# Conditioning products in pairs, and fp32 products of 512 columns cut in two

## The chip, the cores and the metric

The kernel runs on one core of a Trainium2 chip, in one launch. The metric is the device time of that launch in microseconds. TensorE (PE) multiplies; DVE, ACT and POOL work element by element; SP issues most transfers between HBM and the core's memory.

## The reference

A two-layer diffusion backbone on 256 latent and 256 context tokens of width 1024. Layer 0 mixes state-space heads and eight attention heads, layer 1 is a gated MLP over chunks; each is followed by an expert network that picks 16 of 16384 experts for each of eight heads of each token. A conditioning vector gives shift, scale and gate of every sub-layer:

```python
sh1, sc1, g1, sh2, sc2, g2 = jnp.split((cond_lat @ ada_w[layer] + ada_b[layer])[:, None, :], N_MOD, axis=-1)
h_l = _modulate(_rmsnorm(x, norm1_g[layer]), sh1, sc1)
...
x = x + g1 * y_l
x = x + g2 * _peer(_modulate(_rmsnorm(x, norm2_g[layer]), sh2, sc2), ...)
```

`ada_w` is 2 x 1024 x 6144 in fp32, 50 MB, and only two rows (latent and context condition) are multiplied with it.

## The kernel before, in words

The parts follow each other: layer 0's mixer (products into convolution, states and low-rank projections; then attention and state-space outputs; then the output projection), its experts, layer 1's gated MLP, its experts. All heavy products run on TensorE. Large weights come in fp32 tiles `wr` through SP's queue, are split into a high and a low part (`whl`) on ACT and on POOL or DVE, and multiplied in three passes (`mm3`); other products are plain fp32 (`mm`, line 250). A plain fp32 product shows in the profile as two records, each with its own weight load.

The conditioning products are spread through layer 0's mixer. Four tiles `aw` (line 50, `NAW = 4`; 128 x 512, 256 KB each) take turns. `ada_group` (line 494) makes one group of 2048 of the 6144 columns of a layer: 8 slices of the inner dimension (k) by 4 column tiles (t), 32 products, each a tile `aw` against the condition's slice `condT[:, k, :]` of 32 columns. The result of column tile t goes into rows 32t to 32t + 31 of one bank, `ps`, so the four tiles of a k use four different strips of rows. A step issues the transfer of tile i and then multiplies tile i - 3. `adas` (line 728) runs five groups one after the other: group (0,1), (0,2), (1,0), (1,1), (1,2), as (layer, group), all into the same bank; between two groups `ada_tail` adds the bias on DVE, from the bank into `mod` or `mt`. The first group, (0,0), has code of its own: `ada_first`, and `second`, whose last four products read `aw` too. So 164 products read `aw`.

The order on every engine is written when the program is built, by a planner (`schedule`, line 206): each part of the work is a generator that yields conditions; a clock for each engine (`Clock`) adds up costs, and of the generators that are ready the one goes on whose engine's clock is lowest; among equals the first of the list. `at(...)` (line 246) is ready when TensorE's clock has come to the time at which the tiles are there. `ada` is the third of the first list (the mixer's input part) and the first of the second list (attention). Since all clocks are shared, a shift in one place can move work on every engine behind it. Instructions of an engine run in the written order: one that waits holds all that stand behind it on its engine.

In the attention part, four passes work on two heads each. `scores` makes the keys (`kn`, products of `ckh` and `ckl`), the values (`vt`), the queries (`qn`, and `qr` with a rotation on DVE), then for two heads and two token halves the scores, a product of 512 columns with `kn` and one with `krT` into one bank. DVE takes the row maximum (`mx`), ACT the exponential (`pe`), DVE scales it. `values` transposes `pe` (to `pT`) and multiplies it with `vt`. In between, `segments` and `weights` build the state-space part's decay matrices on DVE, eight operations of 128 x 128 at a time (`seg` with `mask_f` or `mask_b`, then `MT`, then `seg` with `dt`), and `outputs` uses them. Eight banks (`pa` and `pb`, four each) go round; a bank that is taken again must have been read.

Plain fp32 products of 512 columns into 128 rows are: the scores, the states (`xw`), the state-space outputs (`hc` and `hs` with `bcT`), broadcasts of one row of `mod`, and in the expert part the products of the rows that tokens share (`rows` with `sc`).

Of the kernel before, what the change touches and what calls it, by code (L numbers as in the profile page):

```python
# [10 lines left out]
F32 = mybir.dt.float32  # L11
# [9 lines left out]
P = 128  # L21
D = 1024
KD = 8
# [174 lines left out]
def tile_backbone(ctx: ExitStack, tc: tile.TileContext, a: dict, out: bass.AP):  # L198
# [3 lines left out]
    clock = Clock()  # L202
    clk = clock.at
    T, V, S, G, Q = (Engine(e, n, clock) for e, n in ((nc.tensor, "T"), (nc.vector, "V"), (nc.scalar, "S"), (nc.gpsimd, "G"), (nc.sync, "D")))
# [28 lines left out]
    class Banks:  # L233
# [5 lines left out]
        def get(self):  # L239
            self.free.sort(key=clock.idle)  # L240
            return self.free.pop(0)
# [4 lines left out]
    def at(*aps):  # L246

        return lambda: clk["T"] + SLACK >= max(clock.ready(x) for x in aps)

    def mm(o, lhsT, rhs, start=True, stop=True):  # L250
        T.matmul(o, lhsT, rhs, start=start, stop=stop)

    def mm3(o, lh, ll, rh, rl, start=True, stop=True):
# [37 lines left out]
    condT = cp.tile([P, KD, 32], F32, name="condT")  # L291
# [120 lines left out]
    def warm(ps, x):  # L412

        while clk["T"] + WARM < clock.ready(x):
            mm(ps[:, :256], identb, ones.bitcast(F16))
# [61 lines left out]
    def features(hh, hl, A, SH, raws):  # L477

        pss, idle = [pa() for _ in range(KD // 2)], pb()
        for t in range(2):  # L480
            warm(idle, diag[t])
            for j in range(KD):
                mm(pss[j // 2][:, j % 2 * 256 + t * P:j % 2 * 256 + (t + 1) * P], xt[t][:, j * P:(j + 1) * P], diag[t])
        for j in range(KD):
            ps, raw, h = pss[j // 2][:, j % 2 * 256:(j % 2 + 1) * 256], raws(j), hh[:, j, :]
            S.activation(h, ps, AF.Identity, scale=A[:, j, 0:1], bias=SH[:, j, 0:1])
            V.tensor_scalar(raw, ps, A[:, j, 0:1], SH[:, j, 0:1], op0=ALU.mult, op1=ALU.add)
            (G if j % 3 == 2 else V).tensor_tensor(hl[:, j, :], raw, h.bitcast(F32), op=ALU.subtract)


    def ada_tail(m, ps):
        V.tensor_tensor(m, ps, m, op=ALU.add)

    def ada_group(l, g, get, bufs, ps):

        units = [(k, t) for k in range(KD) for t in range(4)]
        n = len(bufs)
        for i in range(len(units) + n - 1):
            if i < len(units):
                k, t = units[i]  # L500
                aw = bufs[i % n]
                yield lambda: clk["T"] >= clock.idle(aw)
                Q.dma_start(out=aw, in_=a["ada_w"][l, k * P:(k + 1) * P, g * 2048 + t * 512:g * 2048 + (t + 1) * 512])
            if i >= n - 1:
                k, t = units[i - n + 1]
                aw = bufs[(i - n + 1) % n]
                yield at(aw)
                mm(ps[32 * t:32 * t + 32, :], condT[:, k, :], aw, k == 0, k == KD - 1)
        ada_tail(get(), ps)
        yield  # L510

# [86 lines left out]
    def hybrid(mod):  # L598
# [129 lines left out]
        def adas():  # L728

            yield lambda: "mod1" in done  # L730
            ps = B.get()
            for l, g in ((0, 1), (0, 2), (1, 0), (1, 1), (1, 2)):
                if l == 0:
                    mod.append(mod_load(0, g))
                    yield from ada_group(l, g, lambda: mod[g], awb, ps)
                    done.add(("mod", g))
                    if g == 2:
                        mod2(0, mod, awb[0])
                elif g == 0:
                    yield from ada_group(l, g, lambda: nmod.append(mod_load(1, 0)) or nmod[0], awb, ps)  # L740
                else:
                    mt = ha.tile([P, 512], F32, name="mt", tag="mt")
                    yield from ada_group(l, g, lambda: mod_load(1, g, mt), awb, ps)
                    if g == 2:
                        mod2(1, [None, None, mt], awb[0])
                    S.dma_start(out=ms[g - 1], in_=mt)
            B.put(ps)
# [1383 lines left out]
```

## Time and profile before

| | |
|---|---|
| median of 3 runs | 2077.2 us (2073.23 to 2078.44) |
| the profiled execution | 2073.34 us |
| its span, first to last instruction | 2071.6 us |
| TensorE busy | 1945.0 us, 94% of the span |
| DVE busy | 1368.5 us, 66% |
| landing tiles `aw`: products, records | 164, 328 |
| TensorE idle until a transfer into `aw` had landed | 8.0 us, 11 times |

A profile shows one execution. TensorE's products show as records of which the next may start before the last has ended, so the distance of starts tells what one costs, and the length does not. In the names, `out<-in` stands for what is written and read; for a product the moving operand comes first, then the one held in the array, and 128*32 is the shape of the held operand.

### The profile page before, as it was taken

How to read it: one execution, taken by the hardware profiler on the slowest of the kernel's cores; microseconds unless marked ns; L12 is line 12 of the kernel's file. 1: busy time of each engine (PE TensorE's matmuls, PEld its weight loads, DVE VectorE, ACT ScalarE, POOL GpSimd, SP SyncE). 2: the span in 40 equal slices, each digit the busy share in tenths (PEclk: the TensorE clock that was granted, in tenths of full speed). 3: DMA queues.
4: the chain of work that ended last, by engine and by line, in shares of the span. 5: the costliest groups of instructions: out<-in, count | busy, mean ns of one | idle time of the engine just before them, and what ended most of it. 6: DMA issues, size and time to landing. Idle time of an engine off the chain costs nothing.

```text
span 2071.6 us, 28401 instructions
## 1 busy us (share of the span) xinstructions
PE 1945.0 (94%) x10048; PEld 1574.3 (76%) x10048; DVE 1368.5 (66%) x3634; ACT 540.4 (26%) x1386; POOL 592.2 (29%) x378
## 2 busy tenths in 40 slices
PE   7899999999989999998999998999899999989997
PEld 4565444579878888887877788789688888878786
DVE  3575566247988678878664226579888887776651
ACT  4434343344212122210111154442122221101100
POOL 1324222166011112223221188550111112233210
PEclk9999999999989999999999999999999999989999
DMA  8556664555468668998997364454678788989972
GB/s 302 171 184 215 212 217 145 165 173 184 133 225 293 237 220 310 379 378 293 417 410 260 132 234 153 156 191 128 229 283 307 269 297 298 365 295 412 413 274 82
DMA packets 132489, 519.98 MB, mean 251 GB/s; under 512 B 17222, under 2 KB 17414, under 8 KB 107179
## 3 DMA queue, kind: packets, MB, share of 16 engines
q1 hardware_dynamic: 100320, 312.24, 43.2%
q0 software_dynamic: 30720, 204.69, 25.9%
q8 instruction: 79, 1.29, 0.2%
q10 hardware_dynamic: 1296, 1.15, 0.2%
q14 instruction: 74, 0.61, 0.1%
HBM read 525.60 MB, written 6.91 MB: 257 GB/s over the span
## 4 chain that ended last, share of the span: by engine, by line
PE 55%; DVE 19%; issue 12%; DMA 7%; POOL 5%; ACT 2%; POOLq 0%; SPq 0%; ACTq 0%; DVEq 0%
PE pb L169 28%; PE pa L169 27%; DVE ge L169 6%; DMA wr<-in_dn 4%; POOL rows L169 2%; DVE mk L169 2%; POOL whl L169 2%; DVE acc L169 1%; DVE junk L169 1%; DMA acs<-acc 1%; DVE rows L169 1%; DMA rows<-in_uv,gidx 1%; DVE x L169 1%; DVE oc L169 1%; DVE cacc L169 0%
## 5 line engine op out<-in xcount | busy, mean ns | idle before, releaser
L169 PE MATMUL pa<-phf,wr 128*128 128x256 f32 x2560 | 576.1, 386 | 0.0
L169 PE MATMUL pb<-wr,ge 128*128 128x256 f32 x2560 | 569.4, 383 | 6.5 <-DMA wr<-in_dn 5.4
L169 PEld LDWEIGHTS pb<-wr,ge 128*128 128x128 f32 x2560 | 485.2, 191 | 90.3 <-DMA wr<-in_dn 22.9
L169 PEld LDWEIGHTS pa<-phf,wr 128*128 128x128 f32 x2560 | 492.3, 194 | 67.2
L169 POOL DMA_INDIRECT rows<-in_uv,gidx x200 | 231.7, 1158 | 916.8 <-DVE acc L169 608.0
L169 POOL TENSOR_TENSOR whl<-wr,whl 128x1024 fp32r<-128x1024 f32 (+2 forms) x130 | 314.7, 2434 | 401.9 <-ACT whl L169 392.2
L169 DVE SCALAR_TENSOR_TENSOR junk<-rows,h 128x1024 bf16<-128x1024 f32 x200 | 244.0, 1220 | 85.6 <-DMA rows<-in_uv,gidx 82.5
L169 DVE SCALAR_TENSOR_TENSOR acc<-rows,wt,acc 128x1024 f32<-128x1024 f32 x196 | 250.7, 1279 | 0.0
L169 ACT ACTIVATE act<-act 128x1 f32<-128x1 f32 x206 | 41.7, 203 | 435.6 <-DVE junk L169 420.6
L169 ACT CAST whl<-wr 128x1024 fp32r<-128x1024 f32 (+2 forms) x136 | 136.9, 1018 | 70.7 <-PE pa L169 27.7
L169 ACT ACTIVATE sg<-pa 128x256 f32<-128x256 f32 (+25 forms) x126 | 38.8, 308 | 383.9 <-PE pa L169 375.4
L169 PE MATMUL pb<-oc,o 128*128 128x80 f16 x1024 | 88.2, 255 | 31.8 <-DVE oc L169 31.8
L169 PEld LDWEIGHTS <-o 128*128 128x128 f16 x1024 | 80.8, 118 | 40.9 <-DVE o L169 16.3
L169 PE MATMUL pa<-phh,whl 128*128 128x256 f32 x512 | 96.3, 285 | 2.1 <-DVE phf L169 2.1
L169 PE MATMUL pb<-aw,condT 128*32 128x512 f32 x328 | 93.4, 624 | 5.1 <-DVE mod L169 3.0
L169 DVE SCALAR_TENSOR_TENSOR ge<-pb,ge 128x80 f32<-128x80 f32 (+29 forms) x128 | 36.9, 316 | 78.3 <-ACT ge L169 77.2
L169 PEld LDWEIGHTS pa<-phh,whl 128*128 128x128 f32 x512 | 80.8, 191 | 4.0 <-DVE phf L169 2.5
L169 PE MATMUL pa<-phl,whl 128*128 128x256 f32 x256 | 73.2, 286 | 2.4 <-POOL phl L169 1.3
L169 DVE SCALAR_TENSOR_TENSOR mk<-jp,j,gte 128x128 f32<-128x128 f32 x256 | 72.4, 347 | 1.1
L169 PE MATMUL pb<-whl,cath 128*128 128x512 f32 x192 | 61.8, 400 | 2.0 <-POOL whl L169 1.1
L169 ACT ACTIVATE wt<-act,gsel 128x1 f32<-128x1 f32 x200 | 58.9, 295 | 6.5
L169 DVE TENSOR_TENSOR oc<-eq,pkT 128x640 f16<-128x640 f16 x128 | 57.1, 487 | 2.2
(517 smaller groups left out, 2402.0 us busy)
## 6 DMA issues: line engine op xcount, KB each, us to landing
wr<-in_dn SPq DMA_DIRECT2D x320, 512.0 KB
aw<-in_ada_w SPq DMA_DIRECT2D x164, 256.0 KB
wr<-in_wq SPq DMA_DIRECT2D x32, 512.0 KB
wr<-in_w_out SPq DMA_DIRECT2D x16, 512.0 KB
wr<-in_gm_w_v SPq DMA_DIRECT2D x16, 512.0 KB
wr<-in_gm_w_u SPq DMA_DIRECT2D x16, 512.0 KB
wr<-in_gm_w_out SPq DMA_DIRECT2D x16, 512.0 KB
wr<-in_w_xbc SPq DMA_DIRECT2D x12, 512.0 KB
```

The costliest lines, as they stand in the source:

```text
L169: return f(*args, **kw)
```

## The change

`mm` cuts a plain fp32 product of 512 columns into 128 rows into two of 256 columns of the same bank. `ada_group` goes in steps of two: it waits until two tiles have landed, multiplies both, and then issues the next two transfers into the same two tiles. Two pairs take turns.

```diff
     def mm(o, lhsT, rhs, start=True, stop=True):
+        if rhs.dtype == F32 and lhsT.dtype == F32 and len(rhs.shape) == 2 and rhs.shape[1] == 512 and o.shape[0] == P:
+
+            T.matmul(o[:, :256], lhsT, rhs[:, :256], start=start, stop=False)
+            T.matmul(o[:, 256:], lhsT, rhs[:, 256:], start=False, stop=stop)
+            return
         T.matmul(o, lhsT, rhs, start=start, stop=stop)
...
-        for i in range(len(units) + n - 1):
+        for i in range(0, len(units) + n, 2):
+            if i >= n:
+
+                yield at(*bufs[i % n:i % n + 2])
+                for j in range(2):
+                    k, t = units[i - n + j]
+                    mm(ps[32 * t:32 * t + 32, :], condT[:, k, :], bufs[i % n + j], k == 0, k == KD - 1)
             if i < len(units):
-                k, t = units[i]
-                aw = bufs[i % n]
-                yield lambda: clk["T"] >= clock.idle(aw)
-                Q.dma_start(out=aw, in_=a["ada_w"][l, k * P:(k + 1) * P, g * 2048 + t * 512:g * 2048 + (t + 1) * 512])
-            if i >= n - 1:
-                k, t = units[i - n + 1]
-                aw = bufs[(i - n + 1) % n]
-                yield at(aw)
-                mm(ps[32 * t:32 * t + 32, :], condT[:, k, :], aw, k == 0, k == KD - 1)
+                yield lambda: clk["T"] >= max(clock.idle(x) for x in bufs[i % n:i % n + 2])
+                for j in range(2):
+                    k, t = units[i + j]
+                    Q.dma_start(out=bufs[i % n + j], in_=a["ada_w"][l, k * P:(k + 1) * P, g * 2048 + t * 512:g * 2048 + (t + 1) * 512])
```

The conditioning products themselves, into 32 rows, stay whole. A conditioning group is 16 pairs. What the planner makes of it is seen at three places. The numbers behind the names are those of the built program and differ between the two.

TensorE, second pair of heads, before: conditioning products (`condT`) between the scores (`kn`, `krT`), the transposes (`ident`) and others.

```order
L169 MATMUL pb_127<-aw3_326,condT_82 32x512
L169 MATMUL pb_127<-aw0_323,condT_82 32x512
L169 MATMUL pb_127<-aw1_324,condT_82 32x512
L169 MATMUL pa_124<-kn_1914,qn_2116 128x512
L169 MATMUL pa_124<-krT_336,qr_2173 128x512
L169 MATMUL pb_127<-aw2_325,condT_82 32x512
L169 MATMUL pb_128<-kn_1914,qn_2116 128x512
L169 MATMUL pb_128<-krT_336,qr_2173 128x512
L169 MATMUL pb_129<-ident_69,yt_2043 128x128 x4
L169 MATMUL pb_130<-kn_1914,qn_2116 128x512
L169 MATMUL pb_130<-krT_336,qr_2173 128x512
L169 MATMUL pa_123<-ident_69,pe_2205 128x128 x4
```

The same engine and pair after the change:

```order
L169 MATMUL pb_127<-aw2_325,condT_82 32x512
L169 MATMUL pb_127<-aw3_326,condT_82 32x512
L169 MATMUL pa_123<-kn_1991,qn_2141 128x256 x2
L169 MATMUL pa_123<-krT_336,qr_2223 128x256 x2
L169 MATMUL pa_124<-ident_69,yt_2072 128x128 x4
L169 MATMUL pb_127<-aw0_323,condT_82 32x512
L169 MATMUL pb_127<-aw1_324,condT_82 32x512
L169 MATMUL pb_129<-hs0_329,bcT_339 128x256 x2
L169 MATMUL pa_125<-hc1_328,bcT_339 128x256 x2
L169 MATMUL pb_130<-xlat_337,MT_2094 128x64 x8
L169 MATMUL pb_127<-aw2_325,condT_82 32x512
L169 MATMUL pb_127<-aw3_326,condT_82 32x512
```

Before, runs of three, one and, a few rows later, one; after, each run holds two products, and scores are two instructions each (x2).

DVE, first pair of heads, before: from the rotation of the queries (`qrt`, `qr`) to the first scores' scaling (`pe`).

```order
L169 TENSOR_TENSOR qrt_1809<-pa_123,c2_332 128x256 x2
L169 TENSOR_TENSOR qr_1810<-qrt_1809 128x256
L169 SCALAR_TENSOR_TENSOR seg_1668<-seg_1668,dt_340,cbT_1658 128x128 x8
L169 TENSOR_TENSOR yt_1825<-xlat_337,c2_332 128x512
L169 TENSOR_TENSOR yo_1828<-pa_125,ecum_344 128x512
L169 TENSOR_TENSOR yt_1825<-yt_1825,yo_1828 128x512
L169 TENSOR_TENSOR yo_1834<-pa_126,ecum_344 128x512
L169 TENSOR_TENSOR yt_1825<-yt_1825,yo_1834 128x512
L169 TENSOR_REDUCE mx_1839<-pa_124 128x1
L169 TENSOR_SCALAR mx_1839<-mx_1839 128x1
L169 RECIPROCAL sm_1843<-sm_1843 128x1
L169 TENSOR_SCALAR pe_1842<-pe_1842,sm_1843 128x512
```

DVE after the change, from the first of the additions behind the rotation to the first maximum:

```order
L169 TENSOR_TENSOR yt_1831<-xlat_337,c2_332 128x512
L169 TENSOR_TENSOR yo_1835<-pa_126,ecum_344 128x512
L169 TENSOR_TENSOR yt_1831<-yt_1831,yo_1835 128x512
L169 TENSOR_TENSOR yo_1840<-pb_130,ecum_344 128x512
L169 TENSOR_TENSOR yt_1831<-yt_1831,yo_1840 128x512
L169 SCALAR_TENSOR_TENSOR seg_1727<-seg_1727,cum_341,mask_f_146 128x128 x8
L169 SCALAR_TENSOR_TENSOR seg_1857<-seg_1857,cum_341,mask_b_150 128x128 x8
L169 SCALAR_TENSOR_TENSOR MT_1871<-seg_1727,dt_340,cbT_1666 128x128 x8
L169 SCALAR_TENSOR_TENSOR seg_1857<-seg_1857,dt_340,cbT_1666 128x128 x8
L169 SCALAR_TENSOR_TENSOR seg_1869<-seg_1869,cum_341,mask_f_146 128x128 x8
L169 SCALAR_TENSOR_TENSOR seg_1899<-seg_1899,cum_341,mask_b_150 128x128 x8
L169 TENSOR_REDUCE mx_1917<-pa_123 128x1
```

Between the additions to `yt` and the first maximum six blocks of eight operations (x8) have come in, which stood behind the pair's maxima before.

TensorE, first pair of heads, before: the first scores' bank was `pa_124`, as the maximum's row on DVE shows; here it is taken again, by a key product of the next pair.

```order
L169 MATMUL pa_123<-ident_69,pe_1842 128x128 x4
L169 MATMUL pa_125<-kn_1678,qn_1753 128x512
L169 MATMUL pa_125<-krT_336,qr_1810 128x512
L169 MATMUL pb_127<-aw0_323,condT_82 32x512
L169 MATMUL pb_127<-aw1_324,condT_82 32x512
L169 MATMUL pa_126<-ident_69,pe_1856 128x128 x4
L169 MATMUL pb_127<-aw2_325,condT_82 32x512
L169 MATMUL pa_124<-ckh_335,whl_1750 128x512
L169 MATMUL pa_124<-ckl_334,whl_1750 128x512
L169 MATMUL pa_124<-ckh_335,whl_1750 128x512 x2
L169 MATMUL pa_124<-ckl_334,whl_1750 128x512
L169 MATMUL pa_124<-ckh_335,whl_1750 128x512
```

After the change the first scores' bank is `pa_123` (the maximum's row), and a value product of the next pair takes it:

```order
L169 MATMUL pa_126<-ckh_335,whl_1748 128x512
L169 MATMUL pa_126<-ckl_334,whl_1748 128x512
L169 MATMUL pa_126<-ckh_335,whl_1748 128x512 x2
L169 MATMUL pa_126<-ckl_334,whl_1748 128x512
L169 MATMUL pa_126<-ckh_335,whl_1748 128x512
L169 MATMUL pb_130<-ckh_335,whl_1748 128x512
L169 MATMUL pb_130<-ckl_334,whl_1748 128x512
L169 MATMUL pb_130<-ckh_335,whl_1748 128x512 x2
L169 MATMUL pb_130<-ckl_334,whl_1748 128x512
L169 MATMUL pb_130<-ckh_335,whl_1748 128x512
L169 MATMUL pa_123<-whl_1748,ckh_335 128x256 x2
```

Before, two transposes of `pe` and a run stood ahead of the bank's next use; after, the value product takes the bank ahead of the first transpose.

## Rows read from the trace of the kernel before

**Rows 1.** The page: busy time by engine; the chain that ended last, by engine.
```profile
PE 1945.0 (94%) x10048; PEld 1574.3 (76%) x10048; DVE 1368.5 (66%) x3634; ACT 540.4 (26%) x1386; POOL 592.2 (29%) x378
PE 55%; DVE 19%; issue 12%; DMA 7%; POOL 5%; ACT 2%; POOLq 0%; SPq 0%; ACTq 0%; DVEq 0%
```

**Rows 2.** Stretches: length; busy us of PE, PEld, DVE, ACT, POOL; clock; DMA.
```profile
230.00:300.00 70.00, 68.17 (x310) 34.31 (x308) 51.72 (x138) 30.83 (x54) 15.85 (x7) 1.00 0.66 220
300.00:396.00 96.00, 91.38 (x395) 44.74 (x396) 48.74 (x115) 34.39 (x70) 19.65 (x8) 0.98 0.53 173
```

**Rows 3.** TensorE's timeline: start, length, what, shape, count; key products and one run.
```profile
260.74 0.63 PE L169 MATMUL pa<-ckh,whl 128*128 128x512 f32 x2
...
261.44 0.40 PE L169 MATMUL pa<-ckh,whl 128*128 128x512 f32 x1
261.77 1.05 PE L169 MATMUL pb<-aw,condT 128*32 128x512 f32 x2
262.75 0.50 PE L169 MATMUL pb<-ckh,whl 128*128 128x512 f32 x1
263.08 0.40 PE L169 MATMUL pb<-ckl,whl 128*128 128x512 f32 x1
```

**Rows 4.** TensorE's timeline: a run of four products, eight records.
```profile
109.28 1.06 PE L169 MATMUL pb<-aw,condT 128*32 128x512 f32 x8
110.28 0.50 PE L169 MATMUL pa<-hh,whl 128*128 128x512 f32 x1
```

**Rows 5.** TensorE's timeline: 512 columns, 256 columns, and 256 between other shapes.
```profile
1129.99 10.46 PE L169 MATMUL pb<-rows,sc 128*128 128x512 f32 x24
...
555.71 19.59 PE L169 MATMUL pa<-phf,wr 128*128 128x256 f32 x90
...
312.63 1.99 PE L169 MATMUL pb<-pT,vt 128*128 128x256 f32 x8
314.56 1.05 PE L169 MATMUL pb<-aw,condT 128*32 128x512 f32 x4
```

**Rows 6.** DVE's timeline in the first attention pair, and ACT's exponential.
```profile
231.13 2.19 DVE L169 SCALAR_TENSOR_TENSOR seg<-seg,cum,mask_f 128x128 f32<-128x128 f32 x8 [2.19 <-DMA seg<-cums]
...
249.33 0.68 DVE L169 TENSOR_REDUCE mx<-pa 128x1 f32<-128x512 f32 x1
...
251.65 0.68 DVE L169 TENSOR_REDUCE mx<-pb 128x1 f32<-128x512 f32 x1
...
250.24 0.69 ACT L169 ACTIVATE pe<-pa,mx 128x512 f32<-128x512 f32 x1 [11.19 <-DVE mx L169]
```

**Rows 7.** TensorE's timeline in the first attention pair.
```profile
244.04 1.02 PE L169 MATMUL pa<-kn,qn 128*128 128x512 f32 x2
...
246.04 1.05 PE L169 MATMUL pb<-aw,condT 128*32 128x512 f32 x4
247.03 1.12 PE L169 MATMUL pb<-kn,qn 128*128 128x512 f32 x2
...
249.13 1.13 PE L169 MATMUL pb<-kn,qn 128*128 128x512 f32 x2
...
252.22 2.00 PE L169 MATMUL pb<-xlat,MT 128*128 128x64 f32 x16
254.15 1.05 PE L169 MATMUL pb<-aw,condT 128*32 128x512 f32 x4
```

**Rows 8.** TensorE's timeline: waits, with what ended them in brackets.
```profile
128.72 2.02 PE L169 MATMUL pb<-aw,condT 128*32 128x512 f32 x8 [3.05 <-DVE mod L169]
...
163.75 1.05 PE L169 MATMUL pb<-aw,condT 128*32 128x512 f32 x2 [0.31 <-DMA aw<-in_ada_w]
...
347.60 1.12 PE L169 MATMUL pa<-ident,pe 128*128 128x128 f32 x4 [4.62 <-DVE pe L169]
...
1841.10 0.56 PE L169 MATMUL pa<-cnt,tri 128*128 128x1 f32 x2 [8.83 <-DVE cnt L169]
```

**Rows 9.** SP's timeline: issues to the landing tiles ahead of 163.75.
```profile
160.78 1.75 SPq L169 DMA_DIRECT2D aw<-in_ada_w  x4
```

## The prediction

> **What bounds the kernel now.** I read the page's busy shares and its chain first [rows 1]: TensorE is busy for 94% of the span and makes 55% of the chain; no other engine is above 66%. Then the table of stretches [rows 2]: in the two stretches of the attention part TensorE is busy for 68.2 of 70 us and 91.4 of 96 us, DVE for 51.7 and 48.7, at full granted clock (1.00, the 2.4 GHz level) or 0.98. There the conditioning products of the change stand, between 42 us and 394 us. A microsecond of TensorE work taken out of this part shortens the kernel by a microsecond, as long as no other engine holds TensorE up in its place.
>
> What such a product costs I read from TensorE's timeline. A product of 512 fp32 columns into 32 rows shows as two records. In a stream of products that start 0.23 us apart, (261.44 - 260.74) / 3 with one record left out between, one alone (two records) pushes the stream apart [rows 3]: from the product at 261.44 to that at 263.08 pass 1.64 us, of which two steps of 0.235 us belong to the stream, so the run costs 1.17 us (0.98 from its start to the next product's, 0.19 in slower steps ahead of it and behind it). Two products in a row (four records) take 0.99 us, from 246.04 to 247.03 [rows 7], and four (eight records) 1.00 us [rows 4]: they write four different strips of 32 rows and stream at the same time. So **runs** are paid for, and not products.
>
> **The change, part by part.**
>
> *Fewer runs.* On TensorE's order before, the 164 products that read the four landing tiles stand in 82 runs, 27 of them a single product; after the change in 69, with one single (the last of the second() part, which is not touched). By group of 32 products: 12, 12, 19, 20 and 17 runs before, 11, 11, 13, 16 and 16 after, and two ahead of them in both. 13 runs less x 1.17 us = **-15.3 us**. Removed runs beside other work that waits would give less, but TensorE hardly idles in this part: of its 82 runs the tables of waits show a handful next to one [rows 8].
>
> *The 512-column products cut in two.* The condition takes fp32 products into 128 rows with 512 columns: 24 of the shared rows, 32 of the scores, 20 of the states and their outputs (12 + 8), 16 broadcasts of one row, 92 in all, 184 records. Back to back, 24 records of the shared rows come at (10.46 - 0.59) / 23 = 0.4291 us; records of 256 columns at (19.59 - 0.38) / 89 = 0.2158 us [rows 5]; the subtracted part is the last record's own length. Two of these make 0.4316, 2.5 ns more than one of 512: 184 x 2.5 ns = **+0.5 us**. Weight loads double (184 more), but one of a 256-column stream lies within the record ahead of it, else the step would not be 0.216. Where another tile shape follows, the scores take 2.10 us for two products, or 1.05 each, and four products of 256 columns in the same surroundings 1.93 us, or 0.97 for two [rows 5, 7]; so the bounds are -92 x 0.08 = -7.4 us and, if each extra weight load stood free for the 0.1 us by which a stream is set back at a switch [rows 3], +18.4 us. I take +0.5, from the rows that show the form itself.
>
> The Trainium skill, TensorEngine Tiling (Array Packing), section Instruction Overhead, says that each matmul carries about 60 cycles; at 2.4 GHz that is 25 ns, an estimate of 4.6 us for 184 more records, and the sum below would come to -9.3. The two cadences of this trace contradict it.
>
> *A moved wait on DVE.* The planner's clocks shift, and DVE's order in the first attention pair changes: six blocks of eight seg or MT operations now stand ahead of the first row maximum, where none stood. A block takes 2.18 us [rows 6], six 13.1 us. In the times of before: the maximum began at 249.33 and the exponential of it ended at 251.0, 1.7 us later; now it begins at 262.4 and ends at 264.1. TensorE's order does not wait for it at a transpose but at a bank: after the change the value product takes the bank of the first scores, pa_123. The first scores began at 244.04; one run less stands ahead, so 243.0. From there to the value product: a score pair 2.1, a run 1.1, a pair 2.1, eight MT products 1.9, a run 1.1, two pairs 4.2, twelve key products at 0.235, 2.8 [rows 3, 7]: 258.3. It waits 5.8 us. The third scores' bank is asked for at 264.1 + 1.4 + 1.1 + 0.5 + 1.1 + 0.5 = 268.7 (values, run, transposes, run, transposes); each later maximum comes 2.32 us after the last [rows 6] and two additions lie between, 0.7 each like the maximum, which reads as many columns, so its exponential ends at 264.1 + 4.6 + 1.4 = 270.1: 1.4 us. The next conditioning group must wait for the addition that empties its bank, which stands on DVE behind the fourth maximum (262.4 + 3 x 2.32 + 1.4 = 270.8, its scores ready at 273.1), a weight subtraction of 768 columns (1.0, by columns) and three copies of 512 (0.7 each): it ends at 276.9, and TensorE is there at 270.1 + 1.4 + 1.1 + 0.5 + 1.9 = 275.0 (values, run, transposes, two state products): 1.9 us. Queued behind each wait is all of TensorE. Together **+9.1 us**. From below it is 0 (DVE gets ahead earlier: it idles for 18 of 70 us in this stretch), from above 13.1, the whole of the six blocks.
>
> *Waits that go.* The run at 128.72 waited 3.05 us for the addition of its group [rows 8]; now 24 products at 0.235 and eight transposes at 0.11 stand between the two groups, 6.5 us. At 347.60 TensorE waited 4.62 us for a maximum that came behind the last seg block and additions; that block now comes before the pair's scores, so the last maxima stand behind two additions only. **-7.7 us**, between 0 and that. The waits for landing tiles (0.31 us at 163.75 [rows 8]) I leave as they are: one transfer a product stays, into the same four tiles.
>
> *The weights' transfers* move on SP's queue behind other aw transfers; by TensorE's work between the run that frees the last aw tile ahead of one and its first use, no weight of this part has less than about 20 us, before or after. Cost 0; the cover is those 20 us, and without it a weight's way through the queue, ACT and POOL would show. Later stages: the one-hot products of the expert part move by a product or so; DVE is the one waited for there, and the wait at the listing (8.83 us in the second layer [rows 8]) takes up what is lost ahead of it. Cost 0, bounds -5 and +5.
>
> Sum: -15.3 + 0.5 + 9.1 - 7.7 = -13.4. The profiled execution took 2073.3 us (span 2071.6 and 1.7 around it), so 2059.9; the median of the runs shown is 3.9 us above the profiled execution, which puts the forecast at **2064 us**.
>
> **Rivals.** *None of the old waits goes.* TensorE is faster now and meets the same DVE results later in its own work; a wait at the bank or at the transposes takes the place of each. For it: the DVE wait at 347.60 arose just as the new one does. Against: DVE's own order ahead of the last maxima is shorter. -15.3 + 0.5 + 9.1 = -5.7, and 2071.5: no change that can be told.
>
> *The pair waits for its second half.* A run may start when both halves have landed, and both are issued only when the run that used the tiles is over. Before, the run at 163.75 still waited although its transfer was issued at about 161 [rows 8, 9]. If each of the 45 runs of the last three groups waits 0.5 us, that is 22.5 us: -13.4 + 22.5 = +9, and 2086, slower. From 0.3 us a run it eats the gain. Against: the 45 runs lie over some 166 us, 3.7 us apart, and a tile is used again two runs later, 7.4 us.
>
> *The moved DVE work costs nothing.* If DVE begins its six blocks early enough, the +9.1 falls out: -22.5, and 2055. Against: the blocks stand behind the rotation of the queries, which needs TensorE's last query product.
>
> **How the numbers follow.** 0.60 for the forecast (2058 to 2070 its own range), 0.17 for the old waits that stay, 0.09 for the waits on second halves, 0.14 for the free DVE work. 0.3% is 6.2 us, about what a measurement of this kernel can tell from no change. Faster: 0.14 and nearly all of 0.60, 0.72; within it: the rest of that and 0.17, 0.19; slower: 0.09. The range goes from the last rival to just past no change: 2053 to 2079.
>
> **What would show it.** TensorE's timeline with 69 runs on the landing tiles, a single one among them, each 0.98 us; records of 256 columns of rows,sc at 0.216 us. A wait of some 6 us on ACT pe or DVE at the first value products of the second pair, and none at the last scores. Wrong it is if the summed idle time of TensorE up to 400 us grows by more than 10 us, if waits for aw are above 10 us in all (8.0 before), or if a score pair takes clearly more or less than 2.1 us.

## The result, and the profile after

The changed kernel takes 2065.65 us (median of 6 runs, 2063.17 to 2067.31) against 2076.97 us (6 runs, 2072.95 to 2078.44): ratio 0.9949, 95% interval 0.9936 to 0.9962, or 11.3 us less. The forecast was 2064. The profiled execution took 2064.5 us, with a span of 2062.8. (The granted clock in the tables is a share of full speed: 1.00 is the 2.4 GHz level, 0.50 the 1.2 GHz level.)

The page after, busy time and the chain by engine (before: [rows 1]):

```profile
PE 1935.5 (94%) x10229; PEld 1606.4 (78%) x10229; DVE 1370.5 (66%) x3635; ACT 542.2 (26%) x1380; POOL 596.5 (29%) x377
PE 62%; DVE 17%; DMA 8%; issue 7%; POOL 4%; ACT 2%; SPq 0%; POOLq 0%; ACTq 0%; DVEq 0%
```

TensorE has 181 more records and 9.5 us less busy time. Stretches after the change: busy us of PE, PEld, DVE, ACT and POOL, then granted clock and DMA (before: [rows 2]).

```profile
230.00:300.00 70.00, 60.26 (x303) 37.37 (x301) 55.42 (x153) 28.89 (x51) 22.58 (x7) 0.93 0.58 195
300.00:396.00 96.00, 92.28 (x469) 56.36 (x469) 41.38 (x92) 36.90 (x76) 15.49 (x7) 0.99 0.57 188
```

In the first stretch, where TensorE was busy for 68.2 of 70 us, it is now busy for 60.3, at a clock of 0.93: something new stands in its way there. TensorE's timeline, runs and a split score pair at another place, and the split products of the shared rows (before: [rows 3, 5, 7]):

```profile
300.38 1.05 PE L169 MATMUL pb<-aw,condT 128*32 128x512 f32 x4
301.36 1.13 PE L169 MATMUL pb<-kn,qn 128*128 128x256 f32 x4
302.42 1.13 PE L169 MATMUL pb<-krT,qr 64*128 64x256 f32 x4
303.48 1.05 PE L169 MATMUL pb<-aw,condT 128*32 128x512 f32 x4
304.46 0.66 PE L169 MATMUL pa<-ident,pe 128*128 128x128 f32 x4
...
1116.28 10.52 PE L169 MATMUL pb<-rows,sc 128*128 128x256 f32 x48
```

A pair of conditioning products (x4 records) costs 0.98 us, from 300.38 to 301.36, as a single one did; there are 69 runs. A score pair takes 303.48 - 301.36 = 2.12 us, 2.10 before. 48 records of 256 columns come at (10.52 - 0.38) / 47 = 0.2157 us, as forecast.

TensorE in the first attention pair (before: [rows 7]), with what ended a wait in brackets:

```profile
251.71 0.39 PE L169 MATMUL pb<-ckh,whl 128*128 128x512 f32 x1
258.05 0.80 PE L169 MATMUL pa<-whl,ckh 128*128 128x256 f32 x2 [5.95 <-ACT pe L169]
...
264.38 2.59 PE L169 MATMUL pb<-aw,condT 128*32 128x512 f32 x4 [3.40 <-DMA aw<-in_ada_w]
266.89 1.11 PE L169 MATMUL pa<-ident,pe 128*128 128x128 f32 x4
```

DVE's blocks ahead of the first maximum, from the first to the last of the six and the maximum (before: [rows 6]):

```profile
243.65 2.18 DVE L169 SCALAR_TENSOR_TENSOR seg<-seg,cum,mask_f 128x128 f32<-128x128 f32 x8
...
254.15 2.18 DVE L169 SCALAR_TENSOR_TENSOR seg<-seg,cum,mask_b 128x128 f32<-128x128 f32 x8
256.25 0.68 DVE L169 TENSOR_REDUCE mx<-pa 128x1 f32<-128x512 f32 x1
```

The value product of the second pair waits 5.95 us for the exponential that frees its bank: the wait that was forecast, with 5.8, at the place in the order that was forecast. Behind it, in this execution, comes one that was not: 3.40 us for a landing tile (the runs below show that it does not come each time). SP's own queue over the same time, and what it waited for:

```profile
236.32 0.80 SPq L169 DMA_DIRECT2D aw<-in_ada_w  x2
237.18 21.71 SPq L169 DMA_DIRECT2D seg<-cums  x4
258.98 1.80 SPq L169 DMA_DIRECT2D aw<-in_ada_w  x4
```
```profile
SPq L169 <- POOL MT L169: 12.3, 2, 8.1
SPq L169 <- DVE MT L169: 7.8, 1, 7.8
```

The six blocks bring four seg transfers with them, which stand in a row on SP. Three of these wait, 20.1 us in sum, until an older seg tile has been read, and the conditioning transfers stand behind them until 258.98.

The two waits that were to go are gone: where runs waited 3.05 and 4.62 us [rows 8], the timeline after the change shows no wait in the runs at 130.70 and 137.48 and in the transposes at 347.93.

### The profile page after: what moved, and what is told of

It is laid out like the page before. It is cut to its first block, busy times and chain, and to the rows that moved or that the text cites. A ratio compares the mean times of both kernels' runs of the same rounds, so it can differ in the third digit from the quotient of the medians.

```text
span 2062.8 us, 28777 instructions
## 1 busy us (share of the span) xinstructions
PE 1935.5 (94%) x10229; PEld 1606.4 (78%) x10229; DVE 1370.5 (66%) x3635; ACT 542.2 (26%) x1380; POOL 596.5 (29%) x377
## 4 chain that ended last, share of the span: by engine, by line
PE 62%; DVE 17%; DMA 8%; issue 7%; POOL 4%; ACT 2%; SPq 0%; POOLq 0%; ACTq 0%; DVEq 0%
PE pa L169 32%; PE pb L169 30%; DVE ge L169 6%; DMA wr<-in_dn 6%; POOL whl L169 2%; DVE mk L169 1%; POOL rows L169 1%; DVE rows L169 1%; DVE acc L169 1%; DVE junk L169 1%; DMA aw<-in_ada_w 1%; DVE x L169 1%; DMA acs<-acc 1%; DVE oc L169 1%; DVE seg L169 0%
## 5 line engine op out<-in xcount | busy, mean ns | idle before, releaser
L169 PEld LDWEIGHTS pa<-phf,wr 128*128 128x128 f32 x2560 | 492.0, 194 | 68.2 <-issue 1.1
L169 ACT ACTIVATE sg<-pa 128x256 f32<-128x256 f32 (+23 forms) x126 | 39.6, 314 | 382.6 <-PE pa L169 363.5
L169 PE MATMUL pb<-aw,condT 128*32 128x512 f32 x328 | 79.9, 618 | 4.0 <-DMA aw<-in_ada_w 4.0
L169 ACT ACTIVATE ge<-pa 128x256 f32<-128x256 f32 (+25 forms) x116 | 35.4, 306 | 81.4 <-PE pa L169 81.4
```

Of the source, the lines that this page charges most:

```text
L169: return f(*args, **kw)
```

## The experiments

In each, the time before was measured on the same chip together with the run; ratios are to that time. A trace is one execution. Where two kernels below have the same order in the mixer, their traces show how much one execution differs from another: with the order of before, the first product of the first expert starts at 463.29, 465.18 and 465.86 us; with that of the changed kernel at 450.61 to 457.72 (four traces).

**The split alone**, on the kernel before. The order on DVE, ACT, POOL and SP is that of before, row for row.

```
 def mm(o, lhsT, rhs, start=True, stop=True):
+    (512 fp32 columns, 128 rows: as two matmuls of 256)
     T.matmul(o, lhsT, rhs, start=start, stop=stop)
```

> The kernel before with the 512-column products of 128 rows cut in two, conditioning products one tile at a time as before. The order on every engine is that of before, with two records where one stood. Theory A (the split costs its extra records, 2.5 ns each, 92 x 2): about 0 to +1 us against before, 2077 to 2078. Rival B (the split gives the gain, because a 256-column product lets TensorE switch sooner between tile shapes): -6 to -11 us, 2066 to 2071. Score pairs between other shapes take 2.10 us before; A expects 2.08 to 2.14, B under 2.05.

Measured: 2077.23 us against 2076.47, ratio 1.0007 (0.9997 to 1.0017). A score pair takes 2.12 us, from 297.97 to 300.09, as theory A expects. The split gives nothing; rival B falls.

**The pairs alone**: the changed kernel without the lines above; the other engines' order is that of the changed kernel.

> The changed kernel with the 512-column products whole again; conditioning products in pairs. The order on every engine is that of the changed kernel. Theory A: the whole gain is here, 2064 to 2066, 69 conditioning runs, the waits at the first attention pair (5.9 us for the exponential and 3.4 us for a landing tile) present. Rival B: no gain, 2074 to 2078.

Measured: 2063.72 us, ratio 0.9940 (0.9928 to 0.9953). The gain is the pairs'. The waits at the first attention pair are not those of the changed kernel's trace, though the order is the same: TensorE waits 7.97 us for the exponential and not for a landing tile, and behind it come the two waits that the prediction had put there, at the third scores' bank (1.73 us) and at the boundary of the conditioning group (0.67 us).

```profile
256.92 0.80 PE L169 MATMUL pa<-whl,ckh 128*128 128x256 f32 x2 [7.97 <-ACT pe L169]
...
265.73 0.50 PE L169 MATMUL pb<-whl,ckh 128*128 128x256 f32 x2 [1.73 <-ACT pe L169]
...
272.21 1.05 PE L169 MATMUL pb<-aw,condT 128*32 128x512 f32 x4 [0.67 <-DVE mod L169]
```

The same three waits stand in the traces of two later runs with this mixer order: 6.43, 2.02 and 0.66 us in the changed kernel with aligned expert parts, 7.97, 2.55 and 0.42 us in the same without the split. In none of the three traces does a product wait for a landing tile; only weight loads do, for 2.3 to 2.8 us in all. There SP issues the conditioning transfers about 3.2 us before the value product starts; in the changed kernel's own trace 0.9 us after it.

**Maxima first**: one condition keeps the third seg block behind the first pair's maxima.

```
 for n, (c_, g, d) in enumerate(units):
+    if n == 2:
+        yield lambda: "max0" in done        # set in scores, behind a pair's four maxima
```

> The changed kernel, but the third seg block on DVE may not be placed ahead of the maxima of the first pair of heads: four seg and MT blocks stand ahead of the first maximum, as before the change, where ten stood; 66 conditioning runs instead of 69. Theory A (the six blocks cost the change 5.95 us of wait for the exponential, 3.4 us for the landing tile whose transfer stood behind the seg transfers on SP's queue, about 1.6 us at the group's boundary and some 3 us of half clock behind it, 14 us together; the old wait of 4.6 us at the third pair may come back with its low clock, 7 us): three runs less, 3.3 us, and 14 less 7 to 0: 2049 to 2057. Rival C (a wait for DVE takes the place of each that is removed): 2062 to 2068.

Measured: 2070.32 us, ratio 0.9966 (0.9954 to 0.9979): slower than the changed kernel and above the ranges of both theories, so by the total theory A has failed. The traces say where. Stretches of the attention part, of before, of the changed kernel and of this one, columns as above:

```profile
249.00:256.00 7.00, 7.00 (x34) 3.43 (x34) 4.25 (x13) 2.33 (x6) 0.00 (x0) 1.00 0.36 121
256.00:272.00 16.00, 15.72 (x68) 7.57 (x66) 11.04 (x34) 9.88 (x17) 1.86 (x1) 1.00 0.74 242
```
```profile
249.00:256.00 7.00, 3.10 (x13) 2.17 (x12) 7.00 (x28) 1.89 (x3) 3.74 (x1) 0.90 0.20 76
256.00:272.00 16.00, 10.55 (x45) 5.96 (x46) 9.24 (x24) 10.33 (x19) 2.54 (x1) 0.73 0.56 190
```
```profile
249.00:256.00 7.00, 7.00 (x35) 3.51 (x31) 2.82 (x7) 4.71 (x9) 0.00 (x0) 1.00 0.70 227
256.00:272.00 16.00, 15.55 (x79) 9.76 (x78) 11.70 (x38) 8.11 (x17) 1.84 (x1) 1.00 0.75 243
```

The waits of the first pair are gone, TensorE is busy for 22.55 of 23 us instead of 13.65, and its clock stays at 1.00 where it fell to 0.73. The mixer does end earlier. First product of the first expert part, in this order: before, changed, maxima first:

```profile
463.29 0.39 PE L169 MATMUL pa<-phh,whl 128*128 128x256 f32 x1 [1.07 <-DVE phf L169]
```
```profile
454.09 0.39 PE L169 MATMUL pa<-phh,whl 128*128 128x256 f32 x1 [0.61 <-DVE phf L169]
```
```profile
442.97 0.39 PE L169 MATMUL pa<-phh,whl 128*128 128x256 f32 x1 [1.08 <-DVE phf L169]
```

So 11.1 us were won in the mixer and 15.5 lost behind it. In both experts the one-hot products (`oc,o`) have another order against the products with `phf`, because the planner's clocks stand elsewhere when the expert begins; where they come early, TensorE waits for DVE. The waits of more than 1 us in the first expert behind the first one-hot product, of the changed kernel and of this one:

```profile
619.20 0.24 PE L169 MATMUL pb<-oc,o 128*128 128x80 f16 x1 [2.06 <-DVE oc L169]
662.34 0.24 PE L169 MATMUL pb<-oc,o 128*128 128x80 f16 x1 [1.63 <-DVE oc L169]
693.03 0.24 PE L169 MATMUL pb<-oc,o 128*128 128x80 f16 x1 [1.62 <-DVE oc L169]
```
```profile
607.10 0.24 PE L169 MATMUL pb<-oc,o 128*128 128x80 f16 x1 [1.14 <-DVE oc L169]
619.76 0.24 PE L169 MATMUL pb<-oc,o 128*128 128x80 f16 x1 [1.65 <-DVE oc L169]
...
753.97 0.24 PE L169 MATMUL pb<-oc,o 128*128 128x80 f16 x1 [1.70 <-DVE oc L169]
```

Three against six. With the low clock behind each, the stretch from the first one-hot product to the first product with `ge` takes 256.9 us there and 266.6 here; 4.8 of these 9.7 us are idle time, and up to 4.5 the clock (the length of the stretch times one minus its mean granted clock, 8.0 and 12.5 us).

**Four at once**: steps of four instead of two, in the same four landing tiles.

```
-for i in range(0, len(units) + n, 2):     # and 2 for 4 in the five lines below
+for i in range(0, len(units) + n, 4):
```

> The changed kernel with the conditioning products of the later groups four at a time, all four landing tiles in one step: 42 runs instead of 69. Eleven seg and MT blocks stand ahead of the first maximum. Theory A (runs are paid, 1.1 us each, whether of two or of four; transfers are hidden): -27 x 1.1 = -30 us, less up to 10 us of waits for landing tiles and one more block ahead of the first maximum: 2036 to 2048. Rival D (a run that needs all its tiles landed, issued only when the last run is over, waits for the last of them each time, 1 us or more): -30 + 40 = +10, 2066 to 2080, with waits for landing tiles of over 30 us in sum where the changed kernel has 4.

Measured: 2060.27 us, ratio 0.9914 (0.9899 to 0.9929), between both theories; by the ratios it is 7 us faster than the changed kernel. The mixer ends at 452.70 us in its trace, 1.4 us earlier than with pairs, but that execution took 2062.71 us, 2.4 more than the median. TensorE's and its weight loads' waits for landing tiles, of before, of the changed kernel and of this one (us, times):

```profile
  DMA aw<-in_ada_w: 8.0, 11
```
```profile
  DMA aw<-in_ada_w: 11.4, 9
```
```profile
  DMA aw<-in_ada_w: 18.9, 27
```

27 runs less took 14.0 us of run time away (75.4 to 61.4 us, from the first record of each run to the next product, idle left out) instead of the 26 that 0.95 a run would give, since some 15 of the runs take 1.2 to 4.3 us: part of their tiles land while they run, and some run at the lower clock. TensorE's idle time grew by 10 us (33.8 to 44.0), and the clock lost up to 24 us in sum over 24 to 464 us (8 x (1 - granted clock) over stretches of 8 us, idle time counted too) instead of 15 to 21 in four traces with the order of the pairs. Part of rival D holds, although the landing waits stay under the 30 us that it asked for: a step that needs all its tiles at once waits for the last.

**The expert parts aligned.** To take the experts' order out of the comparison, the planner's clocks are set to one value at the start of each expert part; the instructions get no wait from it. PHASE shifts that value.

```
 def peer(l, mod, a2, sh2):
+    align(PHASE)        # every engine's clock in the planner is set to one common later value
```

From there on the order on DVE and TensorE is the same in the first two of these kernels and in three at a time below, and in maxima first, with another PHASE, but for one operation on DVE.

> The kernel before; the planner's clocks are set to one common value at the start of each expert part, at a fixed phase, so that from there on the order is the same in this and the next three kernels (but for the 512-column products). The mixer's order is that of before. In the runs so far the stretch from the first one-hot product to the first product with ge goes by the order of the one-hot products: 262.2, 261.2 and 260.3 us for one order, 256.9 and 257.3 for a second, 255.1 and 257.6 for a third, 266.6 and 266.0 for a fourth. Theory E (the order alone sets it): here both layers have the second order, so 262.2 + 255.1 becomes 257 + 257, 2077 - 3 = 2074. Rival F (the stretch depends on when the mixer ends or on what is in flight): within 2 us of 2077.

> The changed kernel with the expert parts' order as in the run before this. Theory E: the second layer's stretch falls from 261.2 to 257 us: 2065.7 - 4 = 2061.5, and the difference from the aligned kernel before is the mixer's alone, 9 to 12.5 us. Rival F: 2065 to 2067.

> The third seg block held behind the first pair's maxima, with the expert parts' order aligned. Its mixer ended 11 us earlier than that of the changed kernel (442.97 against 454.09 us) but the two experts took 5.5 and 10.5 us longer than before, in the fourth order of the one-hot products. Theory E: 2061.5 - 11 = 2050.5 (2048 to 2053). Rival F (what the mixer gains is lost in the experts whatever their order): 2060 to 2068.

Measured: 2074.45 us (0.9986, 0.9973 to 0.9999), 2062.30 (0.9936, 0.9919 to 0.9953) and 2048.98 (0.9873, 0.9856 to 0.9890), each within 2 us of theory E. The stretch of the one-hot products takes 256.6 to 257.8 us in all six experts, and rival F falls, by the third of these times above all. The changed mixer alone is worth 2074.45 - 2062.30 = 12.2 us; the profiled mixers end at 465.86 and 453.63 us, also 12.2 apart, which one trace each does not settle to a microsecond (see above). Maxima first gives 13.3 us more.

**Three at a time in six landing tiles**, aligned: `NAW = 6`, steps of three, 49 runs.

> The changed kernel with six landing tiles and the conditioning products of the later groups three at a time; 49 runs instead of 69; four seg and MT blocks ahead of the first maximum; expert parts aligned. Theory A (runs are paid, about 1 us each, and the six blocks ahead of the maxima cost the changed kernel 11 us): 2061.5 - 20 - 11 = 2030.5, 2028 to 2040 with some waits for landing tiles or DVE in place of those removed. Rival G (each removed run gives back its time as a wait for DVE or for a landing tile, as with four at once, where 27 runs less gave 2 us of mixer): 2050 to 2060.

Measured: 2045.72 us, ratio 0.9852 (0.9835 to 0.9870): faster than both kernels, by 16.6 us than the aligned changed one, but only 3.3 us under maxima first, which has 17 runs more. It lies between the ranges of theory A and rival G, and neither holds as it was put. Waits for landing tiles are down to 2.7 us, and the runs' own time falls from 73.0 to 58.7 us. Yet the mixer ends at 439.03 us, where maxima first ends at 438.14. Stretches of the mixer's last part, of maxima first (aligned) and of this kernel:

```profile
240.00:340.00 100.00, 97.47 (x508) 59.71 (x508) 76.11 (x187) 47.24 (x90) 20.95 (x9) 1.00 0.64 204
340.00:440.00 100.00, 90.90 (x452) 68.18 (x451) 39.42 (x74) 42.77 (x76) 46.12 (x22) 0.97 0.52 177
```
```profile
240.00:340.00 100.00, 96.25 (x542) 65.28 (x542) 71.33 (x173) 41.12 (x80) 21.53 (x9) 0.98 0.60 200
340.00:440.00 100.00, 87.35 (x389) 70.50 (x389) 47.66 (x100) 44.44 (x84) 47.90 (x23) 0.86 0.36 121
```

The granted clock is 0.86 in the last 100 us: TensorE waits 3.01 us for `MT` and runs at the lower level for a while after it. Its timeline there:

```profile
368.34 3.62 PE L170 MATMUL pa<-xlat,MT 128*128 128x64 f32 x16 [3.01 <-POOL MT L170]
371.75 3.68 PE L170 MATMUL pb<-pT,vt 128*128 128x256 f32 x8
376.78 0.66 PE L170 MATMUL pa<-ident,yt 128*128 128x128 f32 x4 [1.34 <-ACT yt L170]
```

The records of eight MT products take 3.62 us and those of four value products 3.68, where they took 2.00 and 1.99 at full clock [rows 5, 7]. Over 24 to 464 us, counted as above, the clock costs this kernel up to 24 us and maxima first 8 in this trace, whose execution took 2044.13 us, 4.9 less than the median (mean clock 0.975, in the other four 0.971 or 0.972), and 15 in the trace that was not aligned, whose mixer has the same order. That leaves 9 to 15 us for the clock, against 14 us that the runs gave: much of them, and perhaps all. It is read from few traces; keeping the clock up in this kernel was not tried.

**The split taken out**, of the aligned changed kernel and of three at a time; the other engines' order stays.

> The changed kernel with aligned expert parts (2062.3 us, 0.9936 of before) with the 512-column products whole again; the order on DVE, ACT, POOL and SP is the same. Theory A (the split costs 184 records x 2.5 ns): 2061 to 2063, ratio 0.993 to 0.994. Rival H (each extra weight load stands partly free, up to 0.1 us): 2045 to 2058.

> Three at a time with six landing tiles and aligned expert parts (2045.7 us, 0.9852 of before) with the 512-column products whole again; the order on DVE, ACT, POOL and SP is the same. Theory A: 2044 to 2046. Rival H: 2028 to 2041. If the low clock of its mixer (14 stretches of 8 us below 0.97, 24 us of clock lost in sum, where the maxima-first kernel has 8) comes from its waits, it is there again.

Measured: 2060.22 us, ratio 0.9923 (0.9909 to 0.9937), and 2045.68, ratio 0.9841 (0.9824 to 0.9858): against the split ones 0.0013 and 0.0011 lower. The pairs alone were 0.0009 below the changed kernel, and the split alone 0.0007 above before. None of the four differs from zero by itself; all point one way, at about 0.001 or 2 us for the split. The first of the two times is a little below theory A's range, the second within it, and rival H falls. The low clock of three at a time is there again (up to 24 us lost, 14 and 15 of them from 340 to 440 us, where maxima first loses 3 and 5), so it belongs to the order.

## Why the prediction was right, step by step

*What bounds the kernel* held: the gain of the mixer came to the end undiminished once the experts' order was the same (12.2 us, and 13.3 more with maxima first).

*Fewer runs*, -15.3: the count of 69 is right, and the price nearly so (13 x 1.17 is 15.2, not 15.3). The runs' own time fell from 87.8 to 75.4 us, 12.4 us or 0.95 a run; the 0.19 us of slower neighbours that I had added is not in that figure and could not be told apart.

*The split*, +0.5: about 2 us, within the bounds, and the cadence of the split products is as forecast. The estimate from the Trainium skill, TensorEngine Tiling (Array Packing), section Instruction Overhead, was 4.6 us for the added records; 2 lies between it and mine. The split alone, with at most 3.5 us by its interval (1.0017), speaks against 4.6; the other three comparisons are too wide to tell.

*The moved wait*, +9.1: the step held. The wait at the first scores' bank is 5.95 to 7.97 us in the four traces with this order, for 5.8. In three of them the third scores' bank and the group's boundary follow as forecast, with 1.7 to 2.6 us for 1.4 and 0.4 to 0.7 for 1.9; the sums are 9.1 to 10.9 us. In the fourth, the changed kernel's own, 3.40 us for a landing tile stand in place of these two, and the sum is 9.35. So the size was right, but partly by luck. I had placed all of this 6 to 7 us too late: the first scores start at 236.23 us and the maximum at 256.25, where I had 243.0 and 262.4, and only the distance between them held. I had also left out three things: ACT loads its tables twice, 1.28 us each, ahead of the third exponential; SP's queue, from which the 3.40 us come; and the low clock, up to 5 us from 249 to 280 us. Over the whole mixer the clock loses up to 15 to 19 us in three traces with the order before and 15 to 21 in four with the order after, so no difference can be told there.

The waits for landing tiles, which I had left as they were, are 11.4 us in the changed kernel's trace, past the 10 that I had named as a sign of error; in the other three traces with this order they are 2.3 to 2.8 us, and with the order before 8.0, 4.5 and 8.7. The sign showed in one execution, and not in the kernel. (Of the 8.0 us that the table ahead of the prediction calls idle time of TensorE, 2.0 are that; 6.0 are idle time of its weight loads, which run beside the products.)

Two runs price the six blocks: without them, and with three runs less, the mixer is 11.1 us shorter by the traces, 15.5 when aligned, and 13.3 by the medians. Less 3 for the runs this leaves 8 to 12.5, against 9.1.

*Waits that go*, -7.7: both went. TensorE's idle time from 27 us to the expert still rose, from 30.7 to 33.8 us, in part since the moved wait is the larger.

*Later stages*, 0 with bounds -5 and +5: this was the weak step. In the profiled executions the experts and the second mixer together took 1596.4 us before and 1596.8 after, but that holds about -5 in the first expert and +6 in the second; maxima first lost 16 us there. That these cancel is chance, and the forecast of the total owes this term to it.

The rivals: the old waits did not stay. The wait for a pair's second half is small with pairs and shows with four at once. The moved DVE work is not free, and the kernel without it shows what that rival was worth: about 13 us, of which some 3 are runs.

## What to carry to other kernels

Count runs of a tile shape, not products, and give them landing tiles enough that no step waits for its last one. When a planner writes the order, a change early on moves everything behind it: before judging one, hold the later order fixed, or a gain of 13 us reads as a loss of 4 (maxima first). Compare several traces of one order before a wait that one of them shows is put down to the change. And price a wait on TensorE with the low clock behind it, and with what stands on the DMA queue behind transfers that wait.

## What was not expected of the hardware

- The lower clock level comes behind short waits too, and its price is not small beside theirs: up to 5 us from 249 to 280 us, with 9.35 us of waits. In the changed kernel TensorE waited 5.95 us from 252 us on, and the clock was 0.90 in 249 to 256 us and 0.73 in 256 to 272; four transposes last 1.11 us at 266.89 and 0.66 at 304.46. The Trainium skill, TensorE: Matmul & The Clock Gate, section Loop structure matters more than you think, warns of loops in which TensorE waits for a transfer between its products and then runs cold; here a wait for ACT, behind DVE, and one for POOL (3.01 us, in three at a time) have the same behind them.
- Runs of six products (12 records) take 1.84 us or more until the next product, against 0.99 for most runs of three and 1.00 for most runs of four; this timeline of three at a time shows one of each. Such a run uses two strips of rows twice; runs of five, which use one strip twice, take 1.83 us or more as well.

```profile
66.86 1.06 PE L170 MATMUL pb<-aw,condT 128*32 128x512 f32 x6
73.64 1.91 PE L170 MATMUL pb<-aw,condT 128*32 128x512 f32 x12
```
